# V of the banded and the differential heads: projected with the tokens on the partitions, in place of projecting, copying and transposing

## The chip, the cores and the metric

The kernel runs on one core of a Trainium2 chip. The time is the device time of one execution in microseconds, the median of several runs.

## The reference, cut to what matters

Two blocks of two layers each work on x (512 tokens, 1024 wide). The first is a transformer with two kinds of attention and a gated delta rule; the change doesn't touch it. In the second block each layer has a mixer of four groups (banded attention with grouped queries, a convolution, differential attention, neighbourhood attention) and a SwiGLU. The mixer reads two streams, x (512 tokens) and a context c (256 tokens), projects both with the same matrix, and every attention lets the queries see the keys and values of c too:

```python
def project(h, w_in):
    qa, ka, va, ub, qc, kc, vc, qd, kd, vd = jnp.split(h @ w_in, SPLIT_IDX, axis=-1)
...
def hybrid_mixer(hx, hc, w_in, ...):
    qa, ka, va, ub, qc, kc, vc, qd, kd, vd = project(hx, w_in)
    qa_c, ka_c, va_c, ub_c, qc_c, kc_c, vc_c, qd_c, kd_c, vd_c = project(hc, w_in)
    ...
    y_a = window_gqa(qa, ka, va, ka_c, va_c, sink)
    y_c = diff_out(diff_attention_latent(qc, kc, vc, kc_c, vc_c, lam), subln_g, lambda_init)
    y_d = neighbourhood_attn(qd, kd, vd, kd_c, vd_c, rpb)
```

`va` is 128 columns wide, `vc` and `vd` 256 each. All is float32. The attention needs V with tokens on the partitions: probabilities (transposed, keys on partitions) times V contracts over the keys.

## The kernel before, in words

Activations lie with features on the partitions: h is a pair of tiles [128, 8, tokens], a high part `hh` and a low part `hl`, both fp32r, that sum to the float32 value. A weight is loaded in chunks, and `split` (L170) makes its two parts, `whi` on ACT and `wlo` on DVE. A product in float32 is three matmuls for each of the 8 slices of the contraction: high by high, low by high, high by low (`mm3`, L245 to L247), so 24 in all.

There are two ways to project. `mm_fm` (L249) keeps a 128x128 piece of the weight stationary and moves h, with all tokens as columns: 24 matmuls of 512 columns for x, 24 of 256 for c. The output has features on the partitions. While the counter `fresh` is above zero, one projection in each count is cut in halves of 256 columns, so that it may start on the first half of a norm. `mm_tm` (L259) keeps a 128x128 piece of h stationary (128 tokens) and moves the weight; the output has tokens on the partitions. Each matmul has a weight load of its own (PEld in the profile), in both ways.

V of the three attentions of a mixer is made by `values` (L1473), one call for each pair of heads and stream. It projects with `mm_fm` into a PSUM bank, copies that bank to the SBUF tile `t2b` on ACT (L1482), transposes the copy in pieces of 128 tokens on PE into a second bank (L1485), and evacuates that into V: as a hi and a lo part (L174 on ACT, L175 on DVE), or as one copy where `whole` is set (L1489), which is so for the differential heads. With `turn` (x of the neighbourhood heads) the copy also reorders the tokens by column of the grid (L1480). The banded heads take one call for each stream and layer, the differential and the neighbourhood heads two, for 2 layers: 20 calls. The banded call on c uses the banks "s" of the scores, all others the two banks "dn", which all projections share.

`t2b` is one buffer in the mixers (`self.letters(ap, a=2, b=1, c=1, d=2)`); `axial` (L1161), which rotates q and k, writes it too, from L1167 or L1170 to L1176, and `conv` uses it for its gate (L1381).

The order of the work around it: `mixers` (L1667) writes a list of steps for every unit (a pair of heads): projections of k, V and q of the coming unit, output projections of a done one, and taps of the convolution. `attend` ends with `fill`, which runs steps of the coming unit in proportion to what is done of the current one. A step's weights are loaded two ahead. On top of that the framework's scheduler sets each engine's final order from the dependences, so PE's projections stand among the matmuls of the heads. Before the first unit the steps of the banded heads (keys, V, query) run by themselves. K and q take a way through DRAM (`bounce`, L1443, and `stack_query`, L1457, or `stack_keys`, L1450) before the scores (L1267) can read them. The V of a unit is read by the products with probabilities (L1250, L1257).

```python
    def mm_tm(self, out, w, c0, n, h, t, kt=KD):
        s = slice(t * P, t * P + P)
        self.mm3(out, [(h[0][:, k, s], h[1][:, k, s], *w(k, c0, n)) for k in range(kt)])
```

Of the kernel before, what the change touches and what calls it, by code (L numbers as in the profile page):

```python
# [17 lines left out]
P = 128  # L18
# [123 lines left out]
class Net:  # L142
# [1330 lines left out]
    def values(self, ap, w, c0, name, h, n, whole=False, bank="dn", turn=False):  # L1473

        nc = self.nc
        v = self.t2("b", n)
        if turn:
            nc.scalar.copy(v.rearrange("p (c r) -> p c r", r=8), self.by_column(self.proj(w, c0, h, n, bank)))  # L1480
        else:
            nc.scalar.copy(v, self.proj(w, c0, h, n, bank))  # L1482
        pt = self.psum(bank)[:, :n]
        for t in range(n // P):
            nc.tensor.transpose(pt[:, t * P:t * P + P], v[:, t * P:t * P + P], self.ident)  # L1485
        V = ap.tile([P, n // P, 2, 2, 64], F32R, tag="V" + name, bufs=2, name="V" + name)
        vs = pt.rearrange("p (t h d) -> p t h d", h=2, d=64)
        if whole:
            nc.scalar.copy(V[:, :, :, 0].bitcast(F32), vs)  # L1489
        else:  # L1490
            self.split(V[:, :, :, 0], V[:, :, :, 1], vs)
        return V
# [497 lines left out]
```

## Time and profile before

| | before |
|---|---|
| median of 3 runs | 3399.89 us (3397.77 to 3404.53) |
| profiled execution, time | 3398.42 us |
| its span, first to last instruction | 3396.6 us |
| mean granted clock of TensorE | 0.975 of 2.4 GHz |
| busy, share of the span | PE 95%, PEld 79%, DVE 65%, ACT 37%, POOL 3% |
| first mixer | about 1583 to 2030 us |
| second mixer | about 2640 to 3010 us |

Engines are PE (TensorE's matmuls), PEld (its weight loads, beside the matmuls), DVE (VectorE), ACT (ScalarE), POOL (GpSimd) and SP (SyncE, which issues most DMAs). A busy time of PE counts a matmul from its start to its modelled end, and matmuls overlap, so the distance from start to start says what one costs. "out<-in" are the program's names, and L12 is line 12 of the kernel. In brackets stands how long an engine was idle before an instruction, and what ended that.

### The profile page before, as it was taken

The page shows a single profiled execution, that of the slowest core. Times are in us where ns is not written, and L with a number is a line of the kernel's source. Part 1 is how long each engine was busy: PE and PEld are TensorE (multiplying, and loading weights), DVE is VectorE, ACT ScalarE, POOL GpSimd, SP SyncE. Part 2 cuts the span into 40 slices and gives each one's busy share as a digit, 9 for nine tenths or more (in the row PEclk, how much of TensorE's full clock was granted, in tenths as well). Part 3 has the DMA queues.
Part 4 walks back from the last instruction along what each step waited for, and adds up shares of the span by engine and source line. Part 5 has one row for each costly group of instructions (what it writes and reads, how often), then busy time and mean ns, then how long its engine had stood idle before and what let it go on. Part 6 is the DMA issues. An engine that isn't in the chain of part 4 may idle for free.

```text
span 3396.6 us, 46400 instructions
## 1 busy us (share of the span) xinstructions
PE 3225.8 (95%) x17568; PEld 2673.1 (79%) x17568; DVE 2215.5 (65%) x4553; ACT 1255.7 (37%) x2411; POOL 118.1 (3%) x182
## 2 busy tenths in 40 slices
PE   7998999999999899999899989999999998999998
PEld 4886788887878787887777768888888776778887
DVE  6977655568988676677878777534445876653334
ACT  3566422235443332223644453212123455442222
POOL 4000000000000000000000000000001000000000
PEclk9998999999999999999999999999999999999999
DMA  7645355542122154553342313333332343313332
GB/s 231 171 135 164 115 168 153 163 121 63 38 57 56 51 175 140 171 165 104 117 145 81 106 54 97 114 97 112 118 112 75 110 137 101 106 50 93 99 93 81
DMA packets 479567, 385.54 MB, mean 114 GB/s; under 512 B 20848, under 2 KB 393712, under 8 KB 479344
## 3 DMA queue, kind: packets, MB, share of 16 engines
q1 hardware_dynamic: 479344, 382.58, 37.9%
q8 instruction: 139, 2.28, 0.3%
q14 instruction: 84, 0.69, 0.1%
HBM read 352.09 MB, written 17.83 MB: 109 GB/s over the span
## 4 chain that ended last, share of the span: by engine, by line
PE 42%; DVE 5%; ACT 3%; issue 1%; DMA 1%; POOL 1%; SPq 0%; POOLq 0%; DVEq 0%; ACTq 0%
PE dn L245 6%; PE dn L246 6%; PE dn L247 6%; PE d L246 6%; PE d L247 6%; PE d L245 6%; PE tp L1231 1%; PE s L1267 1%; PE tp L1250 1%; PE tp L1257 1%; DVE cv L1396 1%; ACT pr L1210 1%; DVE wlo L175 1%; PE dn L380 1%; DVE st L1207 0%
## 5 line engine op out<-in xcount | busy, mean ns | idle before, releaser
L174 ACT CAST whi<-raw 128x1024 fp32r<-128x1024 f32 (+1 forms) x399 | 417.2, 1046 | 786.8 <-PE d L247 411.8
L175 DVE TENSOR_TENSOR wlo<-raw,whi 128x1024 fp32r<-128x1024 f32 (+1 forms) x399 | 487.0, 1222 | 268.8 <-ACT whi L174 268.1
L245 PE MATMUL dn<-hh,whi 128*128 128x512 f32 (+1 forms) x1688 | 621.1, 369 | 8.2 <-ACT t2b L1381 4.5
L246 PE MATMUL dn<-hh,wlo 128*128 128x512 f32 (+1 forms) x1688 | 616.2, 366 | 2.2 <-DVE wlo L175 2.2
L247 PE MATMUL dn<-hl,whi 128*128 128x512 f32 (+1 forms) x1688 | 614.7, 366 | 0.0
L245 PE MATMUL d<-hh,whi 128*128 128x512 f32 (+1 forms) x1120 | 400.7, 358 | 0.0
L246 PE MATMUL d<-hh,wlo 128*128 128x512 f32 (+1 forms) x1120 | 400.0, 357 | 0.0
L247 PE MATMUL d<-hl,whi 128*128 128x512 f32 (+1 forms) x1120 | 399.8, 357 | 0.0
L245 PEld LDWEIGHTS dn<-hh,whi 128*128 128x128 f32 x1688 | 323.3, 192 | 56.1 <-ACT t2b L1381 5.1
L246 PEld LDWEIGHTS dn<-hh,wlo 128*128 128x128 f32 x1688 | 323.6, 192 | 44.9 <-DVE wlo L175 2.6
L247 PEld LDWEIGHTS dn<-hl,whi 128*128 128x128 f32 x1688 | 322.5, 192 | 44.7 <-issue 1.8
L313 DVE SCALAR_TENSOR_TENSOR acc<-araw,cond,acc 128x512 f32<-128x512 f32 x322 | 242.3, 752 | 67.3 <-DMA araw<-in_ada_w 35.5
L245 PE MATMUL d<-gh,whi 128*128 128x512 f32 (+1 forms) x696 | 252.3, 363 | 0.0
L246 PE MATMUL d<-gh,wlo 128*128 128x512 f32 (+1 forms) x696 | 250.3, 360 | 0.0
L247 PE MATMUL d<-gl,whi 128*128 128x512 f32 (+1 forms) x696 | 249.3, 360 | 0.0
L245 PEld LDWEIGHTS d<-hh,whi 128*128 128x128 f32 x1120 | 210.7, 188 | 32.6 <-issue 1.3
L246 PEld LDWEIGHTS d<-hh,wlo 128*128 128x128 f32 x1120 | 210.7, 188 | 32.5 <-issue 1.3
L247 PEld LDWEIGHTS d<-hl,whi 128*128 128x128 f32 x1120 | 210.7, 188 | 31.6 <-DVE hl L419 0.9
L245 PEld LDWEIGHTS d<-gh,whi 128*128 128x128 f32 x696 | 131.4, 189 | 22.5 <-ACT gh L174 0.6
L247 PEld LDWEIGHTS d<-gl,whi 128*128 128x128 f32 x696 | 130.9, 189 | 22.7 <-DVE gl L175 0.8
L246 PEld LDWEIGHTS d<-gh,wlo 128*128 128x128 f32 x696 | 131.3, 189 | 21.4
L538 DVE TENSOR_TENSOR t2b<-t2a,d 128x512 f32<-128x512 f32 (+1 forms) x67 | 42.0, 627 | 150.8 <-PE d L247 150.8
(513 smaller groups left out, 5602.6 us busy)
## 6 DMA issues: line engine op xcount, KB each, us to landing
araw<-in_ada_w SPq DMA_DIRECT2D x192, 256.0 KB, 3.8
araw<-in_w_ada SPq DMA_DIRECT2D x192, 256.0 KB, 3.1
raw<-in_ffn_w_in SPq DMA_DIRECT2D x88, 512.0 KB, 4.3
raw<-in_ffn_w_out SPq DMA_DIRECT2D x44, 512.0 KB, 4.4
raw<-in_w_in SPq DMA_DIRECT2D x44, 512.0 KB, 3.9
raw<-in_w_gate SPq DMA_DIRECT2D x44, 512.0 KB, 3.9
raw<-in_w_up SPq DMA_DIRECT2D x44, 512.0 KB, 3.9
raw<-in_w_down SPq DMA_DIRECT2D x44, 512.0 KB, 3.6
```

Source lines behind the costliest of these rows:

```text
L174: nc.scalar.copy(hi, src)
L175: nc.vector.tensor_sub(lo, src, hi.bitcast(F32))
L245: self.nc.tensor.matmul(out, lhsT=lh, rhs=rh, start=j == 0, stop=False)
L246: self.nc.tensor.matmul(out, lhsT=ll, rhs=rh, start=False, stop=False)
L247: self.nc.tensor.matmul(out, lhsT=lh, rhs=rl, start=False, stop=j == n - 1)
L313: nc.vector.scalar_tensor_tensor(st[i], raw, s, st[i], op0=ALU.mult, op1=ALU.add)
L380: nc.tensor.matmul(sums, lhsT=weights(k), rhs=sq, start=k == 0, stop=k == KD - 1)
L538: nc.vector.tensor_mul(y, s, pu[:, :n])
L1210: nc.scalar.activation(pr, s, AF.Exp, bias=st[:, 0:1], accum_out=st[:, 2:3])
L1231: nc.tensor.transpose(tp[:, n * P:(n + 1) * P], pr[:, c:c + P], self.ident)
L1250: nc.tensor.matmul(ps[:64, q0:q1], lhsT=lhs, rhs=pt[sl // 2][0][:, sl % 2, q0:q1].bitcast(F32), start=j == 0, stop=j == nb - 1, skip_group ...
L1257: nc.tensor.matmul(ps[:, q0:q1], lhsT=lhs, rhs=pt[sl // 2][i][:, sl % 2, q0:q1], start=j == 0 and i == 0, stop=j == nb - 1 and i == 1, ski ...
```

## The change

In `values`, a call without `turn` no longer projects with `mm_fm`, copies and transposes. For each piece of 128 tokens it runs `mm_tm`, with h stationary and 128 columns of the weight moving, into the bank that took the transposes before. The evacuation into V is as it was, and the calls with `turn` are too.

```diff
         nc = self.nc
-        v = self.t2("b", n)
         if turn:
+            v = self.t2("b", n)
             nc.scalar.copy(v.rearrange("p (c r) -> p c r", r=8), self.by_column(self.proj(w, c0, h, n, bank)))
-        else:
-            nc.scalar.copy(v, self.proj(w, c0, h, n, bank))
         pt = self.psum(bank)[:, :n]
         for t in range(n // P):
-            nc.tensor.transpose(pt[:, t * P:t * P + P], v[:, t * P:t * P + P], self.ident)
+            if turn:
+                nc.tensor.transpose(pt[:, t * P:t * P + P], v[:, t * P:t * P + P], self.ident)
+            else:
+                self.mm_tm(pt[:, t * P:t * P + P], w, c0, P, h, t)
         V = ap.tile([P, n // P, 2, 2, 64], F32R, tag="V" + name, bufs=2, name="V" + name)
```

## Rows read from the trace of the kernel before

**Rows 1.** The page's head: span, and PE's busy time, share and instructions.

```profile
span 3396.6 us, 46400 instructions
PE 3225.8 (95%) x17568; PEld 2673.1 (79%) x17568; DVE 2215.5 (65%) x4553; ACT 1255.7 (37%) x2411; POOL 118.1 (3%) x182
```

**Rows 2.** Stretches: length; busy us of PE, PEld, DVE, ACT, POOL; clock; DMA; GB/s.

```profile
1583.00:2030.00 447.00, 398.99 (x2349) 325.23 (x2348) 350.56 (x860) 222.84 (x580) 10.64 (x23) 0.95 0.35 102
1660.00:1760.00 100.00, 94.71 (x612) 78.28 (x611) 76.60 (x213) 53.42 (x150) 0.16 (x2) 1.00 0.39 119
2640.00:3010.00 370.00, 330.96 (x1835) 264.36 (x1833) 265.10 (x596) 183.66 (x450) 7.55 (x14) 0.94 0.36 105
2700.00:2790.00 90.00, 83.07 (x514) 68.62 (x514) 69.98 (x177) 47.40 (x128) 0.00 (x0) 0.98 0.38 115
```

**Rows 3.** L1482's copies: count, ns min/median/max, first and last start, forms.

```profile
L1482 ACT COPY t2b<-dn x14: 357/390/587, 1613.8 to 2907.0; 128x256 f32<-128x256 f32 x8, 128x512 f32<-128x512 f32 x6
...
L1482 ACT COPY t2b<-s x2: 372/372/372, 1595.4 to 2664.6; 128x256 f32<-128x256 f32 x2
```

**Rows 4.** Timeline of PE, 2640.67 to 2657.09: start us, duration us, instruction.

```profile
2640.67 0.48 PE L245 MATMUL dn<-hh,whi 128*128 128x512 f32 x1
...
2657.09 0.39 PE L247 MATMUL dn<-hl,whi 128*128 128x512 f32 x1
```

**Rows 5.** Timeline of PE, 1582.68 to 1587.16.

```profile
1582.68 0.28 PE L245 MATMUL dn<-hh,whi 128*128 128x256 f32 x1
...
1587.16 0.28 PE L247 MATMUL s<-hl,whi 128*128 128x256 f32 x1
```

**Rows 6.** Timeline of PE and PEld in a banded head, 1657.60 to 1657.77.

```profile
1657.60 0.22 PE L1257 MATMUL tp<-pth,Vx 128*128 128x128 f32 x1
1657.60 0.19 PEld L1257 LDWEIGHTS tp<-ptl,Vx 128*128 128x128 f32 x1
1657.66 0.27 PE L1257 MATMUL tp<-ptl,Vx 128*128 128x128 f32 x1
1657.71 0.19 PEld L1257 LDWEIGHTS tp<-pth,Vx 128*128 128x128 f32 x1
1657.77 0.33 PE L1257 MATMUL tp<-pth,Vx 128*128 128x256 f32 x1
```

**Rows 7.** Timeline of PE: runs of one-column matmuls, and what starts next.

```profile
2613.21 1.40 PE L404 MATMUL tp<-mean_d,t2a 128*128 128x1 f32 x12
2614.47 0.36 PE L245 MATMUL d<-gh,whi 128*128 128x256 f32 x1
...
2629.13 3.57 PE L404 MATMUL tp<-mean_d,t2a 128*128 128x1 f32 x16 [2.16 <-POOL t2a L399]
2632.56 0.77 PE L245 MATMUL dn<-hh,whi 128*128 128x512 f32 x1
```

**Rows 8.** Timeline of PE around one differential V of x, second mixer.

```profile
2772.86 0.66 PE L1485 MATMUL dn<-c_ident,t2b 128*128 128x128 f32 x4 [1.64 <-ACT t2b L1482]
2774.19 0.38 PE L245 MATMUL dn<-hh,whi 128*128 128x256 f32 x1 [0.68 <-ACT Vx L1489]
```

**Rows 9.** Waits of PE over the span: us in total, times, longest us.

```profile
PE dn L1485 <- ACT t2b L1482: 12.2, 8, 5.6
```

**Rows 10.** Timeline of PE around the banded V of x, first mixer.

```profile
1594.44 0.79 PE L245 MATMUL dn<-hh,whi 128*128 128x512 f32 x1 [3.35 <-ACT t2b L1381]
...
1614.46 1.11 PE L1485 MATMUL dn<-c_ident,t2b 128*128 128x128 f32 x4 [5.55 <-ACT t2b L1482]
1615.23 0.56 PE L245 MATMUL dn<-hh,whi 128*128 128x256 f32 x1
```

**Rows 11.** Timeline of PE: the first scores of the second mixer.

```profile
2691.42 0.36 PE L1267 MATMUL s<-stk 128*128 128x256 f32 x1 [3.34 <-DMA stk<-bounce]
```

**Rows 12.** Stretches inside the one-column runs: PEclk is the third number from the end.

```profile
2613.25:2614.40 1.15, 1.15 (x14) 1.15 (x12) 1.15 (x4) 0.60 (x2) 0.56 (x1) 1.00 0.00 0
2629.20:2632.50 3.30, 3.30 (x16) 3.30 (x17) 3.29 (x10) 2.35 (x6) 0.56 (x1) 0.50 0.54 159
```

## The prediction

> **What bounds the kernel now.** I read the page's first lines for the whole [rows 1], then the stretches of the two mixers, where every changed instruction lies [rows 2]. Over the span PE is busy 95%. In the first mixer it is busy 399 of 447 us and in the second 331 of 370, so 48 and 39 us are left over; but in the two stretches that hold the four V projections of the differential heads it is idle only 5.3 of 100 and 6.9 of 90 us. DVE comes next with 351 of 447. What the reader is to see: PE sets the pace where the change is, and little room is left there to hide more PE work.
>
> **What the change touches.** The line of the copy counts the calls [rows 3]: 14 copies out of dn (8 of 256 tokens, 6 of 512) and 2 out of s (256). So 6 calls on the 512 tokens of x (banded 2, differential 4) and 10 on the 256 tokens of c (banded 2, differential 4, neighbourhood 4) lose their copy; the neighbourhood's 4 calls with `turn` are as before.
>
> **Prices of a matmul.** Durations overlap, so I price by start to start.
> - 512 columns: 73 matmuls of projections start between 2640.67 and 2657.09, 72 steps, 0.228 us each [rows 4].
> - 256 columns: 39 between 1582.68 and 1587.16, 38 steps, 0.118 us [rows 5].
> - 128 columns of this type with a fresh 128x128 load each: no long run exists, only pairs inside the banded heads [rows 6]. The first starts at 1657.60, the second at 1657.66 (0.06 later), the next at 1657.77 (0.11 later). The loads tell why: they start at 1657.60 and 1657.71, 0.11 apart, though the second matmul had begun at 1657.66. So one short matmul slips through because its load ran under the 256 columns before it, and from then on a load takes 0.11.
> - The nearest case of pure load: matmuls of one column with a 128x128 load. Twelve take 1.26 us, 0.105 each [rows 7].
>
> I take **0.110** for the new matmul: its columns need only 0.228 / 4 = 0.057, and behind another short one the load has nothing to hide under. The ends are 0.06 (loads always ahead) and 0.118 (no cheaper than 256 columns).
>
> **The sum, part by part.**
> - x, a call: removed are 24 x 0.228 = 5.47 us and 4 transposes (four span 0.66 us with the last one's tail [rows 8]), each with a load of 128x128, so 0.11 a piece; together 5.91. Added are 4 tiles x 24 = 96 matmuls x 0.110 = 10.56. That is +4.65, for 6 calls +27.9.
> - c, a call: 24 x 0.118 + 2 x 0.11 = 3.05 goes; 2 x 24 x 0.110 = 5.28 comes. +2.23, for 10 calls +22.3. Together **+50.2 us** of PE, 628 more instructions of PE.
> - The wait for the copy: PE waits 12.2 us in 8 places for it [rows 9] (one short one, under 0.1, belongs to a turned call). It goes whole, since the new matmuls read h and w, both long there. What is late next is the PE work behind it, and that only needs a free dn buffer; now one is taken where two were, so the 0.68 us that PE waits for the evacuation of V behind one call [rows 8] goes or shrinks too.
> - The banded call of the first mixer is a case of its own [rows 10]. PE stands 3.35 us before 1594.44 for another reason, and then 5.55 us before 1614.46 for the copy, which waits its turn on ACT and for the one buffer t2b. V of c (+2.23) runs ahead of the first gap and fits in it. V of x ends by 1608.91 now; 4.65 us and the 0.44 of the transposes later it would end at about 1613.9, and the next projection, now at 1615.23, could start there. I price this pair at -1.5 in place of +6.9.
> - The banded call of the second mixer gets no such relief: V lies ahead of the projection of q, and the first scores wait for q's bounce through DRAM [rows 11]. Full price, +6.9, less its gap.
> - ACT loses 16 copies of 0.36 to 0.59 us, some 7 us [rows 3]. PE's waits for them are counted above; beyond those ACT is the idler engine, 223 of 447 us [rows 2], so nothing more is taken off.
> - t2b is single; axial (the rotation of q and k) uses it as well and no longer queues with V. I count this in the wait above. No DMA is added, removed or passed by in the code, and SP's and POOL's queues keep their work. The evacuation of V (a copy, or hi on ACT and lo on DVE) waits for a chain that is longer by 4.65; its readers are the next group's heads, a head's time later, so nothing.
> - `fresh` (L253): one of the four halved projections was V of c in the first mixer; now k of x is halved, 48 x 0.118 for 24 x 0.228, +0.2.
>
> Sum: 50.2, less 8.4 for the first banded pair, less 6.6 for the other waits on the copy, gives 35. While V takes longer on PE, ACT and DVE catch up, and waits behind it shrink; of the 12.2 us that PE idles in the two differential stretches [rows 2] at most 6.6 are waits for copies, so 6 to 12 are left to be filled. I take 8 off: **+27**. The profiled execution took 3398.42 us (span 3396.6), so it would be 3425; the median of the runs lies 1.5 above it, so **3427**.
>
> **A rule beside the rows.** The rows give 0.11 for a short matmul with its load behind another short one, and 0.085 as the mean of a pair [rows 6]. The Trainium skill, page "TensorE: Matmul & The Clock Gate", section "Back-to-back issue gap", says that a stream of load and matmul pairs runs at about 81 ns a matmul at 128 columns. By that figure the working above would end at an estimate of +7, some 3407. No run here shows a stream of this type.
>
> **Rivals.**
> 1. **Loads overlap better in a stream**, at the mean of the pair, 0.085. Then x costs 96 x 0.085 - 5.91 = +2.25 and c +1.03, together 23.8; less 4.8 for the first banded pair, 6.6 for waits and a quarter of the rest: +9, 3409. For it: no row shows three short ones in series. (That is the case that the page above stands for.) Against: the second load of the pair is late by just what one load lasts, and the one-column matmuls do not go below 0.10 [rows 6, 7].
> 2. **The other side: the load stays hidden throughout**, as under the first of each pair, 0.06 a matmul. 96 x 0.06 = 5.76 and 48 x 0.06 = 2.88 are 0.15 a call below what goes, about -2.5 in all, and the wait of 12 goes on top: 3398 - 15, so 3385. It decides from 0.074 a matmul downwards: there 576 + 480 = 1056 new matmuls weigh what goes (66 us) and the 12.4. For it: the first of each pair. Against it: each second one [rows 6], and the one-column case.
> 3. **The mixers wait for something else**: the 35 vanish in the 87 idle us of the two stretches, and DVE, 78% busy in the first, sets the pace [rows 2]. 3399. Against: the idle time lies mostly behind the V projections, in heads with no V beside them.
> 4. **The clock.** At the low level the one-column matmuls take 0.214 each (2629.13 to 2632.56, 16 of them) where the granted clock was 0.50, that is 1.2 GHz, and 0.105 at 1.00 [rows 7, 12]. A V chain that meets the low level would run at 0.21, so a call on x costs 96 x 0.214 - 10.56 = 9.9 us more. PE has more work and fewer gaps around most calls, and the granted clock was 1.00 and 0.98 in the stretches of the differential heads [rows 2], so this hits few: with two such calls +20, 3447.
>
> That the change doesn't do what it says is no rival here: the branch is on `turn`, and the counts are those of rows 3.
>
> **How the numbers follow.** Forecast 0.68; rival 1 0.08, rival 2 0.07, rival 3 0.06, rival 4 0.11. About 0.2% (6.8 us) is what a measurement of this kernel can tell from no change. Faster: rival 2, 0.07. Same: rival 3 and the low tails of the forecast and of rival 1, 0.12. Slower: the rest, 0.81. The range runs from 3405 (below rival 1, a chain cheaper than 0.085 or more hidden) to 3452 (0.118 a matmul adds 8; clock and lost cover add the rest); it leaves out rivals 2 and 3 and the worst of the clock.
>
> **What would show it.** In the changed profile: 18220 matmuls on PE (17568 + 628, and 24 for k of x in halves); 4 copies at the line of the turned calls and none at L1482's; runs of 96 and 48 matmuls of 128x128 forms into dn and s with steps of 0.11 and loads as far apart; no wait of PE for the copy; in the first mixer's opening no stand of 5.55. Steps of 0.06 to 0.085 would prove rows 6 misread; steps of 0.21 with a granted clock of 0.50 would be rival 4; steps of 0.11 with no change in the time would be rival 3. I am wrong outright if the whole gets faster with steps of 0.11.

## The result, and the profile after

The median is 3485.53 us over four runs (3480.54 to 3501.87), against 3400.22 for the kernel before on the same chip: 1.0264 times as long (95% interval 1.0245 to 1.0283). The forecast was 3427, in a range of 3405 to 3452. The sign was right, the size was not: +85 us in place of +27.

The head of the page after answers to [rows 1]:

```profile
span 3478.8 us, 47695 instructions
PE 3292.8 (95%) x18220; PEld 2748.8 (79%) x18220; DVE 2219.0 (64%) x4553; ACT 1251.1 (36%) x2395; POOL 118.0 (3%) x182
```

PE runs the 18220 matmuls that were forecast and ACT lost its 16 copies. Span less PE's busy time is 186.0 us where it was 170.8: PE idles 15 us more, though its waits for the copy are gone.

The price of a matmul, in the banded V of x of the first mixer (timeline of PE after):

```profile
1601.10 0.23 PE L245 MATMUL dn<-whi,hh 128*128 128x128 f32 x1
1601.16 0.28 PE L246 MATMUL dn<-whi,hl 128*128 128x128 f32 x1
1601.27 0.27 PE L247 MATMUL dn<-wlo,hh 128*128 128x128 f32 x1
...
1611.65 0.28 PE L247 MATMUL dn<-wlo,hh 128*128 128x128 f32 x1
1611.77 0.34 PE L245 MATMUL dn<-hh,whi 128*128 128x256 f32 x1
...
1617.49 0.77 PE L245 MATMUL dn<-hh,whi 128*128 128x512 f32 x1 [2.70 <-DVE Vx L175]
...
1630.29 1.19 PE L1267 MATMUL s<-stk 128*128 128x256 f32 x4 [5.32 <-DMA stk<-bounce]
```

From the second matmul to the last are 94 steps in 10.49 us, 0.112 each. The gap of 5.55 [rows 10] is gone and the next projection starts right behind V, at 1611.77. But two later waits now stand in its place: 2.70 for the evacuation of V and 5.32 for the query on its way through DRAM. From the first projection into the banks s to the first score the first mixer takes 44.7 us, where it took 43.5 before.

What happens in the differential heads of the first mixer (the same timeline, later):

```profile
1708.31 0.27 PE L246 MATMUL dn<-whi,hl 128*128 128x128 f32 x1
1711.73 0.77 PE L1231 MATMUL tp<-c_ident,pr 128*128 128x128 f32 x5 [3.15 <-ACT pr L1210]
...
1713.17 0.42 PE L245 MATMUL dn<-whi,hh 128*128 128x128 f32 x1
1713.39 0.42 PE L246 MATMUL dn<-whi,hl 128*128 128x128 f32 x1
...
1733.47 0.41 PE L247 MATMUL dn<-wlo,hh 128*128 128x128 f32 x1
1733.68 0.52 PE L245 MATMUL dn<-hh,whi 128*128 128x256 f32 x1
1734.00 0.41 PE L246 MATMUL dn<-hh,wlo 128*128 128x256 f32 x1
1734.21 0.41 PE L247 MATMUL dn<-hl,whi 128*128 128x256 f32 x1
```

PE stands 3.15 us for a softmax. Within 1.5 us of its next start the steps are twice as long, 0.22 where they were 0.11, and stay so through the rest of the first unit's V. At this level 256 columns cost no more than 128 (0.21).

Stretches after: length; busy us of PE, PEld, DVE, ACT, POOL; granted clock; DMA; GB/s. The first is the first mixer [rows 2], then the hundred microseconds of the differential V, and two V chains, one at each level:

```profile
1584.00:2054.00 470.00, 420.00 (x2579) 353.69 (x2578) 338.85 (x820) 210.21 (x541) 10.44 (x22) 0.93 0.33 97
...
1690.00:1790.00 100.00, 94.16 (x607) 84.71 (x607) 51.23 (x121) 33.91 (x84) 0.16 (x2) 0.88 0.33 98
...
1723.50:1733.40 9.90, 9.90 (x48) 9.90 (x48) 0.00 (x0) 0.00 (x0) 0.00 (x0) 0.50 0.00 0
1755.90:1771.80 15.90, 15.90 (x144) 15.90 (x143) 4.63 (x7) 2.07 (x5) 0.00 (x0) 1.00 0.63 182
```

48 matmuls of V take 9.90 us at a granted clock of 0.50, with PE busy throughout; 144 others take 15.90 at 1.00. So the same chain costs 0.11 or 0.21 a step, by the level that it meets.

PE's waits (us in total, times, longest), of the kernel before and then of after; only those that moved most:

```profile
PE s L1267 <- ACT pr L1210: 5.5, 9, 1.8
...
PE s L1267 <- DMA stk<-bounce: 4.0, 2, 3.3
...
PE tp L1231 <- ACT pr L1210: 3.8, 2, 3.1
PE tp L1231 <- DVE pr L1553: 3.7, 5, 1.8
```

```profile
PE s L1267 <- DMA stk<-bounce: 11.9, 3, 5.3
PE s L1267 <- ACT pr L1210: 10.5, 14, 2.1
...
PE tp L1231 <- ACT pr L1210: 9.9, 4, 3.2
...
PE tp L1231 <- DVE pr L1554: 7.1, 5, 2.2
```

These four rose from 17.0 to 39.4 us. The 12.2 of the copy [rows 9] went, and more came back, on softmax results and on the stacks.

**The account.** I split each span's difference to the profile of before in three: PE's idle time (span less busy); the loss at the low clock, which is half the time that PE had work at 0.50, summed over the trace; and the rest, work at full clock. In before these are 170.8, 66.3 and 3159.5 us. Each row is one profiled execution, and the low clock differs from one execution of a kernel to the next.

| profiled run | span | idle | low clock | work |
|---|---|---|---|---|
| after | +82 | +15 | +14 | +53 |
| banded alone | +7 | -4 | -3 | +14 |
| differential alone | +71 | +8 | +38 | +26 |
| neighbourhood alone | +19 | +5 | +5 | +9 |
| differential, both pairs at once | +8 | +6 | +1 | +1 |
| no copy, no transposes | -26 | -12 | -9 | -5 |
| differential, 256 columns | +24 | -9 | +2 | +31 |
| after, fill 0.45 | +95 | +16 | +29 | +50 |
| after, fill 0.8 | +99 | +13 | +38 | +48 |
| after, 256 columns | +39 | -14 | -4 | +56 |
| differential, V ahead of k | +66 | +10 | +32 | +25 |
| before, copy into t2a | -10 | -2 | -8 | 0 |

### The profile page after: what moved, and what is told of

The parts are those of the page before. It is cut to its first block, busy times and chain, and to the rows that moved or that the text cites. A ratio compares the mean times of both kernels' runs of the same rounds, so it can differ in the third digit from the quotient of the medians.

```text
span 3478.8 us, 47695 instructions
## 1 busy us (share of the span) xinstructions
PE 3292.8 (95%) x18220; PEld 2748.8 (79%) x18220; DVE 2219.0 (64%) x4553; ACT 1251.1 (36%) x2395; POOL 118.0 (3%) x182
## 4 chain that ended last, share of the span: by engine, by line
PE 75%; DVE 13%; ACT 4%; DMA 3%; issue 2%; POOL 1%; SPq 0%; DVEq 0%; POOLq 0%; ACTq 0%
PE dn L245 11%; PE dn L246 11%; PE dn L247 11%; PE d L245 10%; PE d L246 10%; PE d L247 10%; DVE cv L1396 2%; DVE wlo L175 2%; PE tp L1231 1%; PE s L1267 1%; DMA araw<-in_ada_w 1%; PE tp L1250 1%; PE i L1070 1%; PE tp L380 1%; DVE acc L313 1%
## 5 line engine op out<-in xcount | busy, mean ns | idle before, releaser
L245 PE MATMUL dn<-hh,whi 128*128 128x512 f32 (+1 forms) x1584 | 582.9, 369 | 6.9 <-DVE Vx L175 3.2
L246 PE MATMUL dn<-hh,wlo 128*128 128x512 f32 (+1 forms) x1584 | 579.7, 367 | 4.5 <-DVE wlo L175 4.5
L247 PE MATMUL dn<-hl,whi 128*128 128x512 f32 (+1 forms) x1584 | 577.7, 366 | 0.0
L245 PEld LDWEIGHTS dn<-hh,whi 128*128 128x128 f32 x1584 | 302.7, 191 | 51.8 <-issue 6.9
L246 PEld LDWEIGHTS dn<-hh,wlo 128*128 128x128 f32 x1584 | 302.6, 191 | 47.0 <-DVE wlo L175 5.3
L247 PEld LDWEIGHTS dn<-hl,whi 128*128 128x128 f32 x1584 | 301.6, 191 | 41.9 <-issue 0.9
```

Source lines behind the costliest of these rows:

```text
L245: self.nc.tensor.matmul(out, lhsT=lh, rhs=rh, start=j == 0, stop=False)
L246: self.nc.tensor.matmul(out, lhsT=ll, rhs=rh, start=False, stop=False)
L247: self.nc.tensor.matmul(out, lhsT=lh, rhs=rl, start=False, stop=j == n - 1)
```

## The experiments

Ratios below are to runs of the kernel before on the same chip, with 95% intervals; microseconds are medians.

### Each group alone

`values` takes the new branch for one group and the old one, with copy and transposes, for the others:

```diff
+        old = turn or group != "c"
...
-            if turn:
+            if old:
```

> V of the banded heads alone goes the new way (2 calls on x, 2 on c); the differential and neighbourhood heads as before. Theory L (the recorded sum: 0.11 us a matmul, waits on the copy gone, the clock stays up): +5 us against before. Theory K (every group costs its PE time and on top of it a lower clock and new waits, as the changed profile's drift by unit shows): about +12 us.

> V of the differential heads alone goes the new way (4 calls on x, 4 on c). Theory L: +18 us against before. Theory K: +50 us, of which 27 are matmuls; there is a stretch of a V chain at a granted clock of 0.50 with steps of 0.21 us.

> V of the neighbourhood heads on c alone goes the new way (4 calls of 256 tokens). Theory L: +5 us against before. Theory K: +18 us. If the three single groups add up to the +85 of the whole change, the cost is local to each; if they add up to much less, it is made by the groups together.

Banded alone: 3403.9 against 3396.19, 1.0021 (1.0011 to 1.0030), +8. Differential alone: 3462.21, 1.0173 (1.0145 to 1.0201), +66. Neighbourhood alone: 3418.54, 1.0062 (1.0047 to 1.0077), +22. The work at full clock is +14, +26 and +9, beside 13.8, 27.5 and 8.9 by the prices of the prediction. So the loads were priced rightly, and what is missing is idle time and clock, most of it in the differential heads. The three add up to +96, so the cost arises in each group and not by their coming together. Of the differential heads alone four runs of one program took 3445.65, 3459.90, 3464.53 and 3469.65 us at mean granted clocks of 0.972, 0.966, 0.965 and 0.963: the longer the time, the lower the clock.

### The differential V of both pairs at once

The first unit of the group projects V of all four heads, 256 columns moving and all used: half the new matmuls, and no copy or transposes.

```diff
+            for i in range(2):
+                self.mm_tm(ps[:, i * 256:i * 256 + 256], w, 0, 256, h, t + i)
```

> As before, but V of both pairs of differential heads at once, tokens on partitions, h stationary and all 256 columns of the weight moving: 144 matmuls of 256 columns a layer in place of 96 of 512 and of 256 and 24 transposes; 4 copies a layer gone. Theory W (the short moving side is the whole cost; the layout and the missing copy are good): before or 3 to 8 us faster. Theory O (h stationary, or the order that the scheduler makes without the copy, costs by itself): slower than before by 10 us or more, though PE has no more columns to move.

3406.9, 1.003 (1.0021 to 1.0039), +11. PE's work is that of before (+1), the clock loss too (+1), and still it is no gain: idle time rises by 6. Theory W's gain did not come, and theory O's side holds. That the idle time comes because all of V now stands ahead of the first unit, with none left to fill the second, is likely but was not tried by itself.

### No copy and no transposes

V is taken straight from the bank of its projection. It then has its features on the partitions, so the heads compute something else, and only the time is of use.

```diff
-            nc.scalar.copy(v, self.proj(w, c0, h, n, bank))
...
-            nc.tensor.transpose(pt[:, t * P:t * P + P], v[:, t * P:t * P + P], self.ident)
+            pt = self.proj(w, c0, h, n, bank)
```

> As before, but in the 16 calls V is evacuated straight from the projection's bank: no copy, no transposes, and no other matmul in their place (V then lies with features on the partitions, so its contents are others and the output is not the reference's). Theory L (the recorded sum: the 12 us of waits on the copy are saved for good): -17 us against before, 4.8 of them transposes. Theory O (the order of PE is made anew, and the softmax chains behind set the pace; other waits take the copy's place): between -5 and +5 us, with PE's idle time as large as before or larger.

3373.06 against 3394.58, 0.9934 (0.9914 to 0.9955), -22. Idle time falls by 12, just the wait of [rows 9], the low clock costs 9 less, and work falls by the transposes' 5. So the waits for the copy can be saved for good. In after they are not, for another reason than that something else was about to wait anyway.

### The differential heads with 256 columns

As "differential alone", the same number of matmuls and loads, but each moves 256 columns of the weight, and the half that is not needed is left in PSUM. Two more things differ: V's weight comes in pieces of half the contraction and all 256 columns, where it came whole in the contraction and 128 wide, and V of x is evacuated in two copies, for it fills two banks.

```diff
+                self.mm_tm(ps[:, i * 256:i * 256 + 256], w, 0, 256, h, t + i)
+            vs = ps.rearrange("p (t m h d) -> p t m h d", t=2, m=2, h=2)[:, :, m]
...
-            st[w] = self.wchunk(w_in[:, 1024 + 256 * i:1280 + 256 * i])
+            st[w] = self.wchunk(w_in[:, 1024 + 256 * i:1280 + 256 * i], "k" if w == "v" else "col")
```

> As the kernel with the differential heads alone changed, but each V matmul moves all 256 columns of the weight, of which half are thrown away: the same 576 matmuls and as many weight loads, twice the columns. By start to start a matmul costs 0.118 in place of 0.111, +4 us. Theory C (the narrow columns let the clock fall and hold it low): mean granted clock back to 0.975, and some 25 us faster than with 128 columns (+66), so +35 to +42 against before, although PE has more to do. Theory N (the clock falls for the waits alone): as slow as with 128 columns or 4 us slower, clock 0.963 to 0.970.

3418.91, 1.0069 (1.0054 to 1.0084): +24 where 128 columns gave +66. Twice the columns is 42 us faster. The place to see it is one group of transposes (the same of the 528 matmuls at L1231) in the differential units of the first mixer. With 128 columns (timeline of PE):

```profile
1705.89 0.27 PE L246 MATMUL dn<-whi,hl 128*128 128x128 f32 x1
1709.33 1.33 PE L1231 MATMUL tp<-c_ident,pr 128*128 128x128 f32 x5 [3.17 <-ACT pr L1210]
1710.31 0.45 PE L247 MATMUL dn<-wlo,hh 128*128 128x128 f32 x1
1710.56 0.41 PE L245 MATMUL dn<-whi,hh 128*128 128x128 f32 x1
```

With 256:

```profile
1703.42 0.62 PE L1231 MATMUL tp<-c_ident,pr 128*128 128x128 f32 x4
1703.80 0.36 PE L247 MATMUL dn<-wlo,hh 128*128 128x256 f32 x1
```

With 128 columns PE stands 3.17 us, with 229 of the two units' 288 V matmuls behind the transposes in its own order, and then runs at half speed. With 256 it comes there 6 us earlier and does not stand. Over the whole trace 196 of the 576 V matmuls start at the low clock with 128 columns and none with 256.

The timelines show how the two orders part. In the first seven places where both have V matmuls behind the same instruction of the heads, there are 1, 3, 5, 7, 3, 1 and 3 with 128 columns, and 2, 6, 9, 13, 4, 4 and 5 with 256. After and the whole change with 256 columns (below) have the same two sets of counts. With 128 columns PE stands 0.49, 0.18, 0.19 and 0.78 us between 1694 and 1700, though V matmuls are left; with 256 no stand there reaches 0.15. The scores of this softmax come 3.5 us later, and DVE runs seven taps of the convolution before it takes their maximum (L1207), which the softmax needs. With 128 columns (timelines of PE and DVE):

```profile
1703.41 0.80 PE L1267 MATMUL s<-stk 128*128 128x256 f32 x4
...
1703.29 3.61 DVE L1396 SCALAR_TENSOR_TENSOR cv<-pad,cw,cv 128x256 f32<-128x256 f32 x7
1706.81 1.42 DVE L1207 TENSOR_REDUCE st<-s 128x1 f32<-128x640 f32 x2
```

With 256 the maximum comes at once, ahead of the taps:

```profile
1699.90 0.75 PE L1267 MATMUL s<-stk 128*128 128x256 f32 x4
...
1700.87 0.81 DVE L1207 TENSOR_REDUCE st<-s 128x1 f32<-128x640 f32 x1
```

That it is the columns, and not the weight's pieces, has this for it: the kernel before, with pieces as in after, has its 256-column V of c as 2, 6 and 9 in the first three of these places.

### How fast the heads' gaps are filled

`SPEED`, by which `fill` spreads the coming unit's steps over the heads, in the kernel after:

```diff
-SPEED = 0.6
+SPEED = 0.45
```

and 0.8 in the other run.

> The changed kernel with the pace of the filled-in steps at 0.45 in place of 0.6: fewer steps early in each unit, more at its end. Nothing of the work changes. Theory O (part of the loss is the order of PE that the change upsets): the time moves by 8 us or more either way. Theory L: within 5 us of the changed kernel.

> The changed kernel with that pace at 0.8: more steps early in each unit, fewer left at its end. Theory O: moves by 8 us or more, and not the same way as 0.45. Theory L: within 5 us of the changed kernel.

3496.28, 1.0295 (1.0274 to 1.0315), and 3489.34, 1.0274 (1.0243 to 1.0305). Neither is better than after's 1.0264. By the medians 0.45 is some 10 us slower than after and 0.8 some 3; with two runs each, and intervals that overlap after's, that decides nothing between the theories. Work and idle time stay, and the low clock takes 29 and 38 us in their profiles. Neither pace brings the loss back.

### The whole change with 256 columns

Banded, differential and neighbourhood calls as in the 256-column run above.

> The whole change, but each of the new V matmuls of all three groups moves 256 columns of the weight and throws the half that it doesn't need away. Same number of matmuls and loads as after, twice the columns. Theory C (narrow matmuls let the clock fall and keep it down, and leave PE's order with fewer V matmuls in the gaps of the heads): the full-clock work costs some 60 us over before (52 in after, and 1056 steps of 0.118 in place of 0.111), low clock at most +5, idle time 0 to -10; +45 to +65, so 20 to 40 us faster than after. Theory K (the price is that of the loads, and the clock's fall in after belongs to the stretch, not to the width): +85 and 8 more, about +93.

3434.68 against 3397.98, 1.0109 (1.0094 to 1.0124): +37, 48 us less than after, though each V matmul moves twice as much. It lands below the range of theory C, and far from theory K. The differential heads' stretch, to set beside the one of after:

```profile
1690.00:1790.00 100.00, 96.76 (x669) 84.46 (x668) 65.42 (x150) 42.40 (x106) 0.16 (x2) 1.00 0.45 131
```

The clock is 1.00 where it was 0.88, and PE does 669 matmuls in place of 607. Of its 1056 V matmuls 16 start at the low clock, of after's 105. Work is +56, by the steps of 0.118 for 0.112, but idle time is 14 under before, as the saved copies should give, where after had 15 more.

### V ahead of k

"Differential alone" with 128 columns and the list of steps in another order, so that wide projections end it.

```diff
-                    [Step(lambda name=name: maps("k", m, name, None if name == "c" else 1.0), (st["k"], m * P)) for name in order]
-                    + [Step(lambda name=name: value(m, name), (st["v"], m * P)) for name in order]
+                    [Step(lambda name=name: value(m, name), (st["v"], m * P)) for name in order]
+                    + [Step(lambda name=name: maps("k", m, name, None if name == "c" else 1.0), (st["k"], m * P)) for name in order]
```

> Only the differential heads changed, as in the run that gave +66, with one more edit: in the list of steps V comes ahead of k, so wide projections of k and q (512 columns) end the list. Same instructions, other order. Theory P (the place decides: a narrow chain left over at the end of a unit is what meets the fallen clock and holds it): the low clock costs under 10 us in place of 38, the full-clock work stays at +26, idle within 8 of before; +25 to +40. Theory N (narrow matmuls cost that wherever they stand): +55 to +75. If k comes too late for the next scores, idle time rises behind the stacking transfers instead, by up to 10.

3461.94, 1.0191 (1.0177 to 1.0205), +64: theory P falls, and the time lies in theory N's range. In the first mixer the first unit's V now runs almost whole at full clock, 19 of 144 matmuls at the low one; the second's meets it instead (timeline of PE):

```profile
1733.68 0.39 PE L247 MATMUL dn<-hl,whi 128*128 128x512 f32 x1
1734.76 0.66 PE L1189 MATMUL dn<-c_ident,cols 128*64 128x128 f32 x8 [0.69 <-ACT t2a L1165]
1735.94 1.09 PE L1189 MATMUL dn<-c_ident,cols 128*64 128x128 f32 x16 [0.52 <-DVE t2d L1195]
1738.35 0.37 PE L245 MATMUL dn<-whi,hh 128*128 128x128 f32 x1 [1.31 <-DVE parts L178]
1738.51 0.42 PE L246 MATMUL dn<-whi,hl 128*128 128x128 f32 x1
```

and stays there (stretches, the clock third from the end):

```profile
1739.00:1772.60 33.60, 33.60 (x152) 32.07 (x152) 6.15 (x16) 4.79 (x14) 0.00 (x0) 0.50 0.45 128
1773.00:1776.00 3.00, 3.00 (x16) 3.00 (x16) 1.23 (x1) 1.53 (x2) 0.00 (x0) 0.50 0.00 0
```

Here no long stand precedes the fall, only gaps of 0.69, 0.52 and 1.31 us around small transposes. Then PE is busy without a break for 33.6 us, on 152 matmuls of which some 140 are V's, at 0.50. The next work, k with 256 columns, starts at 1773.05 and is back at steps of 0.12 by 1776.1.

### The kernel before, with the copy in another buffer

One word: V's copy goes into one of the two buffers t2a, not into the single t2b.

```diff
-        v = self.t2("b", n)
+        v = self.t2("a", n)
```

> The kernel before, with one word changed: V's copy goes into a buffer of the pair t2a in place of the single t2b. Theory T (the copy of V waits for t2b, which the convolution's gate and the rotation hold): the wait of 5.55 us in the first mixer's opening goes and the others shrink; -4 to -8 us against before. Theory A (the copy waits for its turn on ACT, not for the buffer): no change within 3 us; if the rotation's q now waits for V instead, up to +5.

3387.74 (eight runs) against 3397.98, 0.9969 (0.9959 to 0.9979), -10: more than theory T's 4 to 8, and faster than both kernels. PE's wait for the copy, to set beside [rows 9], and the gap of 5.55 [rows 10] (waits, then timeline of PE):

```profile
PE dn L1485 <- ACT t2a L1482: 3.9, 7, 1.0
```

```profile
1609.55 0.66 PE L1485 MATMUL dn<-c_ident,t2a 128*128 128x128 f32 x4 [0.73 <-ACT t2a L1482]
```

8.3 us of 12.2 are gone, and most of the 5.55 was the buffer, not ACT's turn. Again not all of it stays as time: idle falls by 2, since other waits grow (the stack's from 4.0 to 6.8; 1.6 are new for the turned calls, whose copy moved too), and in this profile most of the gain is 8 us less loss at the low clock.

## Why the prediction was wrong in size

**Right.** The step of 0.110 measured 0.112; rivals 1 and 2 are out, since 0.06 is seen only at the first matmul behind wide ones. The sum of work, 50.4, measured 52.5. The copy's waits went, and the last matmul of the first banded V started at 1611.65 (forecast of its end 1613.9) with the next projection right behind. One reading of [rows 9] was wrong, without effect: none of the eight waits is under 0.5 us, and none is a turned call's.

The Trainium skill, page "TensorE: Matmul & The Clock Gate", section "Back-to-back issue gap", gives about 81 ns a matmul for a stream of load and matmul pairs at 128 columns; here it is 112. The same page's section "LDWEIGHTS (loading the stationary operand)" gives a load as its columns over 1.2, in ns, so an estimate of 107 for 128: at full clock the rows come near that (105 [rows 7] and 112), at 0.50 they don't (214 [rows 7] and 0.21 us above).

**The step that failed** is "While V takes longer on PE, ACT and DVE catch up, and waits behind it shrink ... I take 8 off", together with the 15 taken off for the copies. 23 us of idle time should have gone; PE idles 15 us more instead. That is 38 of the 55 us that separate the profiled run's +82 from +27. The framework orders PE and DVE anew for the narrow matmuls, and in that order softmax results and stacks come late while V stands behind them. The run with 256 columns has the same list of steps and the same number of matmuls, and there 14 us do go. So the saving on the copies was there to be had, and the narrow form undid it. The further 8 came in no run: 14 is about the copies' 15 alone. Of the first banded pair, priced at -1.5, came about +1: the wait for the evacuation of V, which was to go or shrink, is 2.70 there, and the query's way through DRAM takes another 5.32.

**The clock**, rival 4, had the right mechanism and too low a price and chance ("this hits few"). The stretches of before at 1.00 and 0.98 were carried over to the narrow matmuls; in after the stretch is at 0.88, and with 256 columns at 1.00 again. The loss is 14 of the 55 us in the profiled run. That was the fastest of the four runs, with a mean clock of 0.972; the others had 0.966, 0.966 and 0.961 at 3485.42, 3485.64 and 3501.87. With that the two rows sum: 38 + 14 + 2 of work is 55 within rounding.

**Rival 3** (the mixers wait for something else) is out: the work shows in full.

Shown by runs: the form with 256 columns, at equal numbers of matmuls and loads, is 42 us faster in the differential heads and 48 in all three, in idle time and clock. The stand of 3.17 us comes from the order: later scores, and DVE's seven taps ahead of the maximum. Not shown: why the order has fewer V matmuls in the early places when they are narrow (by the stand as many were placed, 59 and 56), and how much the weight's pieces and the two evacuations do beside the columns. 128 columns with those pieces weren't tried, nor the same order with both widths.

## What to carry to other kernels

Turning a projection round, so that it needs no transposes, changes the shape of its matmuls: count loads as well as columns, and where a load lasts longer than the columns it serves, price by the load. Then ask what the narrow chain does if the clock falls ahead of it, since it may run at half speed to its end; twice the columns at nearly the same price was the better form here. Look at the order that the framework makes too, for it changed with the shape, on PE and on DVE. And before work is moved to save a wait, try the smallest cure of the wait itself: one word, another buffer, gave 10 us here.

## What the runs showed of the hardware

In these traces a PE that is busy without a break does not by that alone come back to full clock: 152 matmuls, most with 128 columns and a load each, ran 33.6 us at 0.50, and 48 such 9.9 us in after; 3 us of 256-column matmuls behind the 152 were followed by steps of 0.12, those of full clock. The Trainium skill, page "TensorE: Matmul & The Clock Gate", part "The HAM clock gate", ties full speed to a PE that is kept busy; these rows disagree. Its section "HAM oscillation — how this bites in real kernels" lets thin products suffer by waits for DMA and advises to order the loop so that PE does not wait between, or to pad the thin side. PE waited for no DMA in these chains, and the form with 256 columns did help.

Nor does the narrow chain have to bring the clock down: 144 in a row ran 15.9 us at 1.00. And at the low level a matmul with 128 columns and its load costs as much as one with 256, 0.21 us a step, so there the second 128 columns are free.
